# New duration estimates and earlier weight loads in the list schedule of a two-layer flow-matching backbone

## Chip, cores and metric

The kernel runs on one NeuronCore of a Trainium2 chip. The metric is the time of one execution on the device in microseconds (us), the median of several runs; lower is better. The engines are named as in the profile: PE multiplies matrices, DVE and ACT work on vectors and activations, POOL is hardly used, and SP issues every transfer (DMA) of the kernel.

## The reference

Two layers work on 1024 latent tokens and 256 context tokens of width 1024, in float32. Cut to what matters here:

```python
for l in range(DEPTH):                       # DEPTH = 2
    mod = silu(c) @ w_ada[l] + b_ada[l]      # shift, scale, gate; mod_c the same from c_ctx
    h  = rmsnorm(x,  norm_g[l]) * (1 + scale)   + shift
    hc = rmsnorm(xc, norm_g[l]) * (1 + scale_c) + shift_c
    if l % 2 == 1: h = to_col_major(h)       # the 64-wide grid, column by column
    p  = h  @ w_in[l]                        # 1024 x 3600
    pc = hc @ w_in[l]                        # last layer: only the columns of group A
    o_ctx, s_f, s_b = gdn_bidir(pc[..., :A_COLS], 0, 0, ...)
    o_lat, _, _     = gdn_bidir(p[..., :A_COLS], s_f, s_b, ...)
    y = mixer_output(o_lat, p, ...)          # groups A to D, gated, then @ w_out[l]
    x = x + gate * y                         # and xc likewise, but not in the last layer
return rmsnorm(x, final_g)
```

`gdn_bidir` is group A, a gated DeltaNet run forwards and backwards. In chunks of 64 tokens it forms, for each head, a 64x64 lower triangular matrix, inverts it (`tinv`), and then scans over the chunks with a 64x64 state. Group B is a short convolution, group C a convolution of 31 taps with a LayerNorm, group D a gate that mixes the tokens within chunks of 128.

## The kernel before

**Dense work.** Most of PE's time goes to `h @ w_in` and to the output projection, in tiles of 128x128 by 512 columns. The operands are split into a high and a low part, so that each product of a latent tile takes three matmuls (high by high, high by low, low by high). In the names of the trace `hh` and `hl` are the two parts of h, `w` holds the two parts of a block of weights, `r` is the raw block of 512 KB as it was loaded, and `mm` is the accumulator in PSUM. ACT casts `r` into the high part of `w`, DVE subtracts to get the low part. There are two buffers for `r` and two for `w` (`CAPS`); the blocks of the context rows are split into `u` buffers as well. The generator `dense` (its inner function `pump`) loads blocks ahead and splits them, in an order that the strings `ORDER` (layer 0) and `ORDER1` (layer 1) give.

**Group A.** For each set of chunks, PE forms the products of the pair matrices (accumulators `sc` and `ax`, constant operands `Lf` and `Lb`, one for each direction), DVE and ACT bring them into form in `b` buffers, and SP stores them to a scratch in DRAM (`zd`) in many small transfers. The inversion reads them back (`u<-zd`) with another layout and solves row by row on DVE: an alternation of `b<-u` and `u<-u,b`, whose width grows from 30 to 240 columns and shrinks again. There are two groups of it in the latent part. The result goes out to `zb`, comes back as `b<-zb`, is transposed, and `ax<-b,b` on PE begins the preparation of the scan (`ax_1275` in layer 1). The scan then runs chunk by chunk. Group D's gate has `u_1256<-u_1105` shuffles, small transfers from one buffer into another.

**What sets the order.** No instruction is issued where it is written. The whole program is recorded through stand-ins of the engines (`Engine`, `Program.add`), 11,657 operations, and `Program.schedule` puts them in order. It goes through time with one clock for each engine, takes the engine that can start an operation first and there, among the operations that are ready by its own reckoning, the one with the lowest priority number. That number is the place in the written program less a boost (`nc.boost`): 800 for the scan, 600 for the convolutions and for the split of weights (`AHEAD_SPLIT`), 300 for the pair matrices (`AHEAD_GDN`), 0 for the inversion (`AHEAD_INV`). The durations come from `estimate`; an issue on SP has a fixed price in `Program.add`. Some operations may go to ACT or DVE; the schedule chooses by its own clocks. Buffers are granted in the order of the program. Then the operations are emitted, and each engine works them off strictly in that order. Since all of them are issued by one call in `add`, every instruction has that line in the profile (L215).

Of the kernel before, what the change touches and what calls it, by code (L numbers as in the profile page):

```python
# [46 lines left out]
AHEAD_SCAN, AHEAD_GDN, AHEAD_INV, AHEAD_CONV, AHEAD_H, AHEAD_SPLIT = 800, 300, 0, 600, 0, 600  # L47
# [32 lines left out]
class Program:  # L80
# [60 lines left out]
    def estimate(self, eng, method, out, ins, args, kw):  # L141
        acc = kw.get("accum_out") is not None
        n = max(self.cols(out), max([self.cols(x) for x in ins[:1]] or [0]))
        ps = any(str(x.space) == "MemoryType.PSUM" or "PSUM" in str(x.space) for x in ins)
        ptr = sum(1 for x in ins if self.cols(x) == 1) if n > 1 else 0
        if eng == "PE":
            if method == "transpose":
                return 0.12
            lhsT, rhs = ins[0], ins[1]
            n, m, k = self.cols(rhs), self.cols(lhsT), lhsT.shape[0]  # L150
            if "r" in str(rhs.dtype).split("float32")[-1]:
                return max(0.107, n / 2400.0 + 0.0133)
            if m <= 64 or k <= 64:
                return max(0.116, 0.01 + n * 4 / 2400.0) / (4 if self.quads else self.side_by_side(k, m))
            return max(0.214, n * 4 / 2400.0) if n > 16 else 0.4
        if eng == "ACT":
            return (0.051 if ps else 0.093) + n / 1200.0 + 0.093 * (ptr + acc)
        if eng == "DVE":
            if method == "reciprocal":
                return 0.07 + n * 0.00625  # L160
            if method in ("tensor_scalar", "tensor_copy") and not ps:
                return 0.069 + n / 1920.0 + 0.06 * ptr
            return 0.069 + n / 960.0 + 0.06 * ptr
        if method == "memset":
            return 0.036 + n * 0.00083
        return 0.15 + n * 0.0021
# [20 lines left out]
    def add(self, calls):  # L187
        isap = lambda x: hasattr(x, "ap") and hasattr(x, "offset")
        eng, method, f, args, kw = calls[0]
        aps = lambda args, kw: ([args[0]] + ([kw["accum_out"]] if kw.get("accum_out") is not None else []),  # L190
                                [x for x in args[1:] if isap(x)] +
                                [v for k, v in kw.items() if k != "accum_out" and isap(v)])
        outs, ins = aps(args, kw)
        op = Op()
        i = len(self.ops)
        op.prio, op.users, op.ready, op.need, op.finish = i + self.boost, [], 0.0, 0, None
        op.alts, op.dma, op.area, op.mode = {}, 0.0, 0.0, None
        if eng == "PE":
            side = lambda x: 32 if x <= 32 else 64 if x <= 64 else P
            op.mode, op.area = (P, P), 1.0  # L200
            if method != "transpose":
                k, m = side(ins[0].shape[0]), side(self.cols(ins[0]))
                op.mode, op.area = (k, m), k * m / (P * P) * self.side_by_side(k, m)
        if eng == "SP":
            n = args[0].size() if callable(args[0].size) else args[0].size
            run = min(x.ap[-1][1] if x.ap[-1][0] == 1 else 1 for x in (args[0], args[1]))
            op.dma = n * 4 / 360e3 * (1.0 if run >= 128 else 2.0)
        for e, m, fn, ar, k in calls:
            table = None
            if e == "ACT" and m == "activation":  # L210
                func = ar[2] if len(ar) > 2 else k.get("func")
                table = self.TABLE.get(str(func).split(".")[-1])
            o, n = aps(ar, k)
            cost = 0.475 if e == "SP" else self.estimate(e, m, o[0], n, ar, k)
            op.alts[e] = ((lambda fn=fn, ar=ar, k=k: fn(*ar, **k)), cost, table)  # L215
        deps, tiles = set(), set()
        for w, aps in ((False, ins), (True, outs)):
            for a in aps:
                name = a.name
                if "PSUM" in str(a.space):  # L220
                    m = self.region(a)[2]
                    lo, hi = ((m & -m).bit_length() - 1) // 512, (m.bit_length() - 1) // 512
                    reg = (0, 128, (2 << hi) - (1 << lo))
                elif name in self.slots or "DRAM" in str(a.space):
                    if name not in self.slots and not name.startswith(self.DRAM_OWN):
                        continue
                    reg = self.region(a)
                else:
                    continue
                if name in self.slots:  # L230
                    tiles.add(name)
                h = self.hist.setdefault(name, [])
                keep = []
                for e in h:
                    j, jw, (p0, p1, m) = e
                    if j == i:
                        keep.append(e)
                        continue
                    hit = p0 < reg[1] and reg[0] < p1 and (m & reg[2])
                    if hit and (w or jw):  # L240
                        deps.add(j)
                        if w and reg[0] <= p0 and p1 <= reg[1] and not (m & ~reg[2]):
                            continue
                    keep.append(e)
                keep.append((i, w, reg))
                self.hist[name] = keep
        if self.joined is not None and eng == "PE":
            deps.add(self.joined)
            self.joined = None
        op.deps, op.tiles = deps, sorted(tiles)  # L250
        for t in tiles:
            self.tileops.setdefault(t, []).append(i)
        self.ops.append(op)
# [213 lines left out]
class Block:  # L467
# [375 lines left out]
    def dense(self, items):  # L843

        n = len(items)
        raws, ws = {}, {}
        st = {"l": 0, "s": 0}

        def pump(i):
            while True:  # L850
                s, moved = st["s"], False
                if s < min(i + 4, n) and s in raws:
                    it = items[s]
                    if self.room(it.pool)():
                        w = self.take(it.pool, [P, 2] + it.shape, F32R)
                        self.nc.boost -= AHEAD_SPLIT
                        self.split(w[:, 0], w[:, 1], raws.pop(s))
                        self.nc.boost += AHEAD_SPLIT
                        self.free("r")
                        ws[s] = w  # L860
                        st["s"] += 1
                        moved = True
                q = st["l"]
                if q < min(i + 6, n) and self.room("r")() and (items[q].cond is None or items[q].cond()):
                    raws[q] = r = self.take("r", [P] + items[q].shape)
                    items[q].load(r)
                    st["l"] += 1
                    moved = True
                if not moved:
                    return  # L870

        for i, it in enumerate(items):
            pump(i)
            while i not in ws:
                yield lambda: (st["l"] > i or items[i].cond is None or items[i].cond()) and \
                    (i not in raws or self.room(it.pool)())
                pump(i)
            for k, v in enumerate(it.run(ws[i])):
                if k % 8 == 0:
                    pump(i)  # L880
                yield v
            del ws[i]
            self.free(it.pool)
# [1285 lines left out]
```

## Time and profile before

| | before |
|---|---|
| median of 3 runs | 1415.69 us (1413.28 to 1418.06) |
| profiled execution | 1418.21 us |
| its span | 1416.1 us, so 2.1 us lie around it |
| mean granted clock of TensorE | 0.943 |
| PE, DVE, ACT busy | 1277.3, 986.6, 544.9 us |
| instructions on DVE; on ACT | 2112; 917, of them 87 table loads |

PE is busy for 90% of the span. Its idle time, 139 us, lies in a few places: the start up to 40 us, the context part of layer 0 (80 to 165 us), the middle of layer 0 where its inversion and scan start (420 to 520 us), and the same place of layer 1 (1090 to 1170 us). Elsewhere PE runs nearly without a gap. The granted clock is given as a share of 2.4 GHz; 0.5 is the lower level, 1.2 GHz.

### The profile page before, as it was taken

How to read it: one execution, taken by the hardware profiler on the slowest of the kernel's cores; microseconds unless marked ns; L12 is line 12 of the kernel's file. 1: busy time of each engine (PE TensorE's matmuls, PEld its weight loads, DVE VectorE, ACT ScalarE, POOL GpSimd, SP SyncE). 2: the span in 40 equal slices, each digit the busy share in tenths (PEclk: the TensorE clock that was granted, in tenths of full speed). 3: DMA queues.
4: the chain of work that ended last, by engine and by line, in shares of the span. 5: the costliest groups of instructions: out<-in, count | busy, mean ns of one | idle time of the engine just before them, and what ended most of it. 6: DMA issues, size and time to landing. Idle time of an engine off the chain costs nothing.

```text
span 1416.1 us, 27022 instructions
## 1 busy us (share of the span) xinstructions
PE 1277.3 (90%) x10888; PEld 1003.2 (71%) x10888; DVE 986.6 (70%) x2112; ACT 544.9 (38%) x917; POOL 11.9 (1%) x76
## 2 busy tenths in 40 slices
PE   6886699999988899999998999989998759999997
PEld 3875577986766655568886778978666646678886
DVE  4787969998855755573376669899776677784454
ACT  3876632254633122132154444343455303231221
POOL 1000000000000000000000000000000000000000
PEclk9997799999996889999999999999999779999999
DMA  9646332322447466573233332334226535132832
GB/s 310 182 108 183 108 89 62 88 46 58 104 105 172 121 178 193 179 223 104 90 112 109 114 104 63 67 81 101 62 50 147 136 85 127 51 105 89 262 84 56
DMA packets 310386, 166.75 MB, mean 118 GB/s; under 512 B 150174, under 2 KB 294902, under 8 KB 310262
## 3 DMA queue, kind: packets, MB, share of 16 engines
q1 hardware_dynamic: 310262, 165.03, 42.9%
q8 instruction: 85, 1.39, 0.4%
q14 instruction: 39, 0.32, 0.1%
HBM read 124.32 MB, written 35.42 MB: 113 GB/s over the span
## 4 chain that ended last, share of the span: by engine, by line
PE 52%; DVE 20%; DMA 12%; SPq 7%; ACT 5%; issue 4%; DVEq 0%; ACTq 0%; POOL 0%; POOLq 0%
PE mm L215 37%; DVE u L215 10%; PE sc L215 10%; SPq L215 7%; PE ax L215 5%; DVE b L215 5%; DMA x<-u 3%; DMA r<-in_w_in 3%; DVE w L215 2%; ACT b L215 1%; DMA u<-zd 1%; ACT L215 1%; DMA zd<-b 1%; ACT u L215 1%; DMA u<-in_x 1%
## 5 line engine op out<-in xcount | busy, mean ns | idle before, releaser
L215 PE MATMUL mm<-hh,w 128*128 128x512 f32 x1664 | 553.9, 407 | 6.8 <-ACT g L215 4.2
L215 PEld LDWEIGHTS mm<-hh,w 128*128 128x128 f32 x1664 | 316.1, 192 | 92.0 <-issue 20.8
L215 PE MATMUL mm<-hl,w 128*128 128x512 f32 x832 | 338.8, 407 | 1.5 <-issue 1.5
L215 PE MATMUL mm<-u,w 128*128 128x512 f32 (+1 forms) x1320 | 264.9, 359 | 13.9 <-ACT w L215 8.7
L215 PEld LDWEIGHTS mm<-u,w 128*128 128x128 f32 x1320 | 222.0, 195 | 48.1 <-ACT w L215 8.9
L215 DVE SCALAR_TENSOR_TENSOR u<-u,pv,u 128x1024 f32<-128x1024 f32 (+1 forms) x172 | 202.7, 1187 | 1.3 <-ACT u L215 0.6
L215 PEld LDWEIGHTS mm<-hl,w 128*128 128x128 f32 x832 | 159.9, 192 | 41.1 <-issue 9.4
L215 ACT CAST w<-r 128x1024 fp32r<-128x1024 f32 x88 | 92.5, 1052 | 249.5 <-PE mm L215 177.0
L215 DVE TENSOR_TENSOR w<-r,w 128x1024 fp32r<-128x1024 f32 x88 | 107.5, 1222 | 40.1 <-ACT w L215 39.8
L215 ACT ACT_TABLE_LOAD x87 | 111.6, 1283 | 21.4 <-DMA zd<-b 11.3
L215 DVE TENSOR_TENSOR u<-u,b 128x256 f32<-128x256 f32 (+26 forms) x246 | 90.1, 387 | 28.1 <-DMA u<-in_x 17.9
L215 ACT ACTIVATE b<-u 128x512 f32<-128x512 f32 (+1 forms) x71 | 42.5, 610 | 66.5 <-DVE u L215 45.5
L215 PE MATMUL mm<-u,u 128*128 128x256 f32 (+1 forms) x384 | 58.7, 303 | 5.7 <-ACT u L215 4.3
L215 DVE TENSOR_TENSOR b<-u 128x198 f32<-128x198 f32 (+24 forms) x180 | 56.9, 331 | 8.5 <-DMA u<-zd 6.9
L215 PEld LDWEIGHTS mm<-u,u 128*128 128x128 f32 x384 | 52.0, 201 | 9.0 <-ACT u L215 4.7
L215 PE MATMUL sc<-ident,b 128*128 128x128 f32 (+1 forms) x139 | 27.5, 322 | 25.2 <-ACT b L215 10.2
L215 PE MATMUL mm<-u,hh 128*128 128x272 f32 x256 | 48.5, 289 | 0.0
L215 PEld LDWEIGHTS sc<-v,u 64*64 64x64 f32 x1184 | 34.4, 140 | 19.6 <-DVE v L215 11.2
L215 PE MATMUL sc<-v,u 64*64 64x64 f32 x1184 | 42.9, 228 | 5.0 <-issue 4.0
L215 ACT COPY v<-sc 128x256 f32<-128x256 f32 x36 | 13.4, 372 | 78.6 <-PE sc L215 69.4
L215 ACT ACTIVATE b<-sc,mod,modG 128x128 f32<-128x128 f32 x86 | 35.0, 456 | 19.4 <-PE sc L215 11.0
L215 PEld LDWEIGHTS sc<-ident,b 128*128 128x128 f32 (+1 forms) x139 | 18.9, 163 | 32.6 <-ACT b L215 13.5
(273 smaller groups left out, 1455.6 us busy)
## 6 DMA issues: line engine op xcount, KB each, us to landing
r<-in_w_in SPq DMA_DIRECT2D x90, 512.0 KB
u<-in_w_ada SPq DMA_DIRECT2D x16, 1024.0 KB
u<-in_x SPq DMA_DIRECT2D x16, 512.0 KB
r<-ylat SPq DMA_DIRECT2D x16, 512.0 KB
ylat<-g SPq DMA_DIRECT2D x24, 256.0 KB
u<-in_w_out SPq DMA_DIRECT2D x12, 512.0 KB
at<-b SPq DMA_DIRECT2D x36, 128.0 KB
u<-at SPq DMA_DIRECT2D x18, 256.0 KB
```

The source lines that it names most:

```text
L215: op.alts[e] = ((lambda fn=fn, ar=ar, k=k: fn(*ar, **k)), cost, table)
```

## The change

Two things change, and no operation is added or taken away. First, the durations that the schedule reckons with: an ACT instruction costs 0.155 or 0.19 us (from PSUM or not) plus its columns, where it cost 0.051 or 0.093; a one-column DVE instruction 0.155 us; a DVE `tensor_tensor` of 129 to 256 columns in SBUF 0.4 us; a PE transpose 0.11 us, or 0.03 for at most 64 rows, where it was 0.12; and an issue on SP 0.62 us, where it was 0.475. Second, the load of a raw block of weights is boosted by 600 places, as its split was already.

```diff
             if method == "transpose":
-                return 0.12
+                return 0.11 if ins[0].shape[0] > 64 else 0.03
...
         if eng == "ACT":
-            return (0.051 if ps else 0.093) + n / 1200.0 + 0.093 * (ptr + acc)
+            return (0.155 if ps else 0.19) + n / 1200.0 + 0.05 * ptr + 0.093 * acc
         if eng == "DVE":
+            if n == 1:
+                return 0.155
             if method == "reciprocal":
                 return 0.07 + n * 0.00625
+            if method == "tensor_tensor" and not ps and 128 < n <= 256:
+                return 0.4
...
-            cost = 0.475 if e == "SP" else self.estimate(e, m, o[0], n, ar, k)
+            cost = 0.62 if e == "SP" else self.estimate(e, m, o[0], n, ar, k)
...
                     raws[q] = r = self.take("r", [P] + items[q].shape)
+                    self.nc.boost -= AHEAD_SPLIT
                     items[q].load(r)
+                    self.nc.boost += AHEAD_SPLIT
```

The effect is a new order on every engine. 104 operations also change between ACT and DVE: DVE has 24 more in all, ACT 24 fewer, and the table loads on ACT go from 87 to 81. Three places matter below, the third of them on two engines. In the names the first number is the buffer's own; the line is L215 before and L219 after, since four lines were added above it.

SP at the very start of the program, before (`whh` and `whl` are the halves of `w_ada`, `r_38` and `r_40` the first raw blocks of weights):

```order
1 L215 DMA b_6_99<-in_c 8x128
2 L215 DMA b_6_99<-in_c_ctx 8x128
3 L215 DMA whh_104<-in_w_ada 128x8x256 x2
4 L215 DMA u_11_106<-in_ctx 128x1024 x2
5 L215 DMA whh_104<-in_w_ada 128x8x256
```

and after:

```order
1 L219 DMA r_38_133<-in_w_in 128x4x16
2 L219 DMA r_38_133<-in_w_in 128x4x256
3 L219 DMA r_40_135<-in_w_in 128x4x16
4 L219 DMA r_40_135<-in_w_in 128x4x256
5 L219 DMA b_6_99<-in_c 8x128
6 L219 DMA b_6_99<-in_c_ctx 8x128
7 L219 DMA whh_104<-in_w_ada 128x8x256 x2
8 L219 DMA u_11_106<-in_ctx 128x1024 x2
9 L219 DMA whh_104<-in_w_ada 128x8x256
10 L219 DMA r_42_137<-in_w_in 128x8x128
```

The first two blocks (four transfers, 1.1 MB) went from behind the third load of `whl` to the head of the queue, and `r_42` and `r_44` (512 KB each) from behind all of `w_ada` to a place ahead of six of its eight loads.

SP in the context part of layer 0, around the loads of `r_201` and `r_210`, before:

```order
52 L215 DMA zd_175_272<-b_176_273 64x2x64 x2
53 L215 DMA zd_175_272<-b_183_280 128x2x64
54 L215 DMA zd_175_272<-b_183_280 64x2x64 x2
55 L215 DMA u_118_215<-u_118_215 32x4x32 x6
56 L215 DMA u_85_182<-in_x 128x1024
57 L215 DMA r_201_298<-in_w_in 128x8x128
58 L215 DMA r_210_307<-in_w_in 128x8x128
```

and after:

```order
46 L219 DMA r_180_277<-in_w_in 128x8x128
47 L219 DMA r_201_298<-in_w_in 128x8x128
48 L219 DMA r_210_307<-in_w_in 128x8x128
49 L219 DMA u_85_182<-in_x 128x1024
50 L219 DMA zd_175_272<-b_176_273 128x2x64
51 L219 DMA zd_175_272<-b_176_273 64x2x64
```

The two loads now stand ahead of the first stores of pair matrices; single issues counted, they moved forward by 29 places.

SP at the end of the pair matrices of layer 1, before the change (`zd_1187` and `zd_1214` are the scratch of the first and second inversion group):

```order
448 L215 DMA u_1186_1285<-zd_1187_1286 32x32x32
449 L215 DMA r_1252_1351<-in_w_in 128x8x128
450 L215 DMA u_1256_1355<-u_1105_1204 32x16x32 x2
451 L215 DMA u_1186_1285<-zd_1187_1286 32x32x32
...
487 L215 DMA zd_1214_1313<-b_1241_1340 64x2x64
488 L215 DMA u_1271_1370<-at_1185_1284 128x512
489 L215 DMA zd_1214_1313<-b_1241_1340 64x2x64
490 L215 DMA u_1186_1285<-zd_1214_1313 32x32x32
```

and after:

```order
477 L219 DMA zd_1214_1313<-b_1241_1340 64x2x64 x2
478 L219 DMA u_1186_1285<-zd_1187_1286 32x32x32 x2
479 L219 DMA r_1278_1377<-in_w_in 128x8x128
480 L219 DMA b_1274_1373<-zd_1187_1286 32x8x32 x4
481 L219 DMA u_1186_1285<-zd_1187_1286 32x32x32 x2
482 L219 DMA u_1256_1355<-u_1105_1204 32x16x32 x8
483 L219 DMA u_1186_1285<-zd_1214_1313 32x32x32 x2
```

The four loads of the first inversion group and eight shuffles of group D stood among the stores of the second group; with one `ylat` store these thirteen issues now stand behind the last store, so that both inversion groups get their data at the end.

PE at the last set of pair matrices of layer 1, before:

```order
3185 L215 MATMUL sc_1235_1334<-b_1237_1336,Lf_15_110 128x256
3186 L215 MATMUL sc_1235_1334<-b_1237_1336,Lb_16_111 128x256
3187 L215 MATMUL mm_1269_1368<-hl1_941,w_1251_1350 128x512
3188 L215 MATMUL mm_1269_1368<-hh1_940,w_1251_1350 128x512
3189 L215 MATMUL mm_1279_1378<-hh1_940,w_1258_1357 128x512
```

and after:

```order
3209 L219 MATMUL mm_1308_1407<-hh1_940,w_1277_1376 128x512 x2
3210 L219 MATMUL sc_1235_1334<-b_1237_1336,Lf_15_110 128x256
3211 L219 MATMUL sc_1235_1334<-b_1237_1336,Lb_16_111 128x256
3212 L219 MATMUL mm_1308_1407<-hl1_941,w_1277_1376 128x512
3213 L219 MATMUL mm_1308_1407<-hh1_940,w_1277_1376 128x512 x2
```

All dense matmuls of the block `w_1258` and the first of `w_1277` now stand ahead of this set. Between its `Lb` product and the first product of `ax_1275` there were 122 dense matmuls of 512 columns, now there are 62; the place of `ax_1275` itself, counted in work ahead of it on PE, is the same.

## Rows read from the trace of the kernel before

**Rows 1.** The page: busy time of the engines, and the chain's shares by engine.
```profile
PE 1277.3 (90%) x10888; PEld 1003.2 (71%) x10888; DVE 986.6 (70%) x2112; ACT 544.9 (38%) x917; POOL 11.9 (1%) x76
...
PE 52%; DVE 20%; DMA 12%; SPq 7%; ACT 5%; issue 4%; DVEq 0%; ACTq 0%; POOL 0%; POOLq 0%
```

**Rows 2.** Windows: stretch, length, engines busy, granted clock, DMA share, GB/s.
```profile
0.00:40.00 40.00, 26.90 (x198) 16.05 (x199) 17.14 (x70) 16.46 (x33) 3.75 (x36) 1.00 0.97 304
...
400.00:440.00 40.00, 32.97 (x249) 25.89 (x249) 14.88 (x26) 10.99 (x13) 0.00 (x0) 0.81 0.50 109
440.00:480.00 40.00, 35.81 (x158) 28.51 (x157) 36.12 (x124) 10.43 (x14) 0.31 (x2) 0.85 0.64 169
480.00:520.00 40.00, 32.93 (x659) 21.51 (x657) 20.32 (x52) 8.70 (x21) 0.00 (x0) 0.79 0.55 140
...
1160.00:1200.00 40.00, 34.04 (x865) 26.25 (x866) 29.61 (x73) 13.06 (x28) 0.00 (x0) 0.85 0.49 125
```

**Rows 3.** PE timeline, context part: start, length, matmul, [idle before it <- releaser].
```profile
85.61 0.50 PE L215 MATMUL mm<-u,u 128*128 128x256 f32 x2 [3.10 <-ACT u L215]
...
120.34 0.80 PE L215 MATMUL mm<-u,w 128*128 128x256 f32 x2 [8.65 <-ACT w L215]
122.36 0.80 PE L215 MATMUL mm<-u,u 128*128 128x256 f32 x2 [1.23 <-ACT u L215]
```

**Rows 4.** SP timeline in the context part: start, length of the issues, transfers.
```profile
109.65 3.86 SPq L215 DMA_DIRECT2D u<-u  x6
...
114.19 1.06 SPq L215 DMA_DIRECT2D r<-in_w_in  x2
```

**Rows 5.** The chain that ended last: a load of weights at two places.
```profile
39.67 5.92 DMA r<-in_w_in
...
114.67 6.58 DMA r<-in_w_in
```

**Rows 6.** The window of 10 us behind the longest wait of the context part.
```profile
120.00:130.00 10.00, 8.43 (x57) 7.99 (x57) 8.05 (x21) 5.35 (x12) 0.00 (x0) 0.61 0.53 140
```

**Rows 7.** SP timeline at the start: the first loads of weights.
```profile
25.46 2.03 SPq L215 DMA_DIRECT2D r<-in_w_in  x4
```

**Rows 8.** PE timeline in layer 1, from the pair matrices to the scan's preparation.
```profile
1093.48 1.03 PE L215 MATMUL sc<-b,Lf 128*128 128x256 f32 x2 [4.98 <-DVE b L215]
...
1102.47 0.59 PE L215 MATMUL sc<-b,Lb 128*128 128x256 f32 x2
...
1103.83 0.62 PE L215 MATMUL mm<-hh,w 128*128 128x512 f32 x2
...
1104.52 0.62 PE L215 MATMUL mm<-hh,w 128*128 128x512 f32 x2
...
1161.56 1.18 PE L215 MATMUL ax<-b,b 32*32 32x32 f32 x64 [12.20 <-DVE b L215]
```

**Rows 9.** SP timeline in layer 1: last store of pair matrices, and what follows.
```profile
1122.79 0.58 SPq L215 DMA_DIRECT2D zd<-b  x1
1123.47 2.23 SPq L215 DMA_DIRECT2D u<-zd  x1
...
1130.88 3.35 SPq L215 DMA_DIRECT2D b<-zd  x4
```

**Rows 10.** The chain in layer 1: a load for the inversion.
```profile
1134.77 4.53 DMA u<-zd
```

**Rows 11.** DVE timeline, inversion: first group begins, second begins, first ends, second ends.
```profile
1106.42 0.21 DVE L215 TENSOR_TENSOR b<-u 128x30 f32<-128x30 f32 x1 [4.96 <-DMA u<-zd]
...
1139.33 0.21 DVE L215 TENSOR_TENSOR b<-u 128x30 f32<-128x30 f32 x1 [1.92 <-DMA u<-zd]
...
1149.32 0.23 DVE L215 TENSOR_TENSOR u<-u,b 128x58 f32<-128x58 f32 x1
...
1165.33 0.19 DVE L215 TENSOR_TENSOR u<-u,b 128x30 f32<-128x30 f32 x1
```

**Rows 12.** The page, costliest groups: an ACT activation of 512 columns.
```profile
L215 ACT ACTIVATE b<-u 128x512 f32<-128x512 f32 (+1 forms) x71 | 42.5, 610 | 66.5 <-DVE u L215 45.5
```

## The prediction

> **What bounds the kernel now.** The page comes first. PE is busy for 1277 of 1416 us, and the chain that ended last runs through PE for 52%, through DVE for 20%, through transfers and their issue for 19% [rows 1]. So for most of the span PE's own work is the bound, and a new order can only change the 139 us in which PE waits. Reordering does not shorten PE's work, except where it keeps the clock at its upper level.
>
> The windows tell where these waits are [rows 2]. At the start (0 to 40 us) PE is busy for 26.9 us, and the DMA engines are 97% busy at 304 GB/s: transfers set the pace there. In the middle of layer 0 (400 to 520 us) PE idles for 120 - 32.97 - 35.81 - 32.93 = 18.3 us, and the granted clock is 0.79 to 0.85, between the two levels of 1.2 and 2.4 GHz. The PE timeline then gives the waits of the context part one by one [rows 3]: 3.10, 8.65 and 1.23 us, 13.0 us together, each for a cast or split of a block of weights. The reader should see behind the 8.65 us a transfer that was issued too late. SP issued the two loads at 114.19 us, behind six shuffles that took 3.86 us, 0.64 us each [rows 4], and one load took 6.58 us on the chain [rows 5]. Behind that wait the granted clock over 10 us is 0.61 [rows 6].
>
> The last big wait is in layer 1. PE idles for 12.20 us ahead of the scan's preparation at 1161.56 us, for data that come out of the inversion [rows 8]. From there PE works nearly without a gap to the end, so the time of this one matmul decides the time of the kernel.
>
> **The change part by part.** No work is added or taken away, so each term below is a change of PE's idle time, or of the time of the matmul at 1161.56 us. The sum is made against the profiled execution (1418.2 us), which lies 2.5 us above the median of the runs.
>
> *Start.* Before, the first four transfers of weights were issued at 25.46 us [rows 7]. They now lead the queue. They are 1.1 MB, at 304 GB/s [rows 2] 3.6 us, by which the first part of w_ada comes later. Two more loads (1.05 MB, 3.4 us) go ahead of six of the eight loads of w_ada. On the other side the load that stood on the chain for 5.92 us at 39.67 us [rows 5] is long done. The ends are -2.3 us (3.6 less 5.9) and +7.1 us (both delays in full); I take +4, because everything of the first 40 us waits for w_ada, and the row with 97% says that no bandwidth is free.
>
> The Trainium skill, DMA: Bandwidth & Descriptors, section Queues, rings and completion order, says that each DMA engine takes descriptors in the order of its ring. By that rule what is first in the queue delays all behind it in full, and this part would cost the larger delay. The trace speaks for something in between: the load of 512 KB took 5.92 us where its bytes alone would take 1.7 at 304 GB/s, so transfers in flight share the engines.
>
> *Context part.* The two late loads move from behind the stores of pair matrices to before them, by 29 issues, and the three pairs after them by 12 to 40. Of the 13.0 us I take 10 away; the loads of the first wait, at 85.6 us, move less (17 issues). With the wait of 8.65 us goes the slow clock behind it: 8.43 us of work at 0.61 [rows 6] would take 5.1, so at most 3.3 us; I take 2, since part of that work waits for other things. The ends are 0 and 16.3 us.
>
> *Other gaps.* An activation of 512 columns takes 610 ns [rows 12]. The old formula reckons 0.093 + 512/1200 = 0.52 us, the new one 0.62; an issue on SP takes 0.64 [rows 4] where 0.475 was reckoned. The list placed work on PE where it thought that inputs were ready, and they were not. What a truer list can get back is at most the 18.3 us in 400 to 520 us and the 4.98 us at 1093 us [rows 8], 23.3 us in all, and possibly nothing, since the order of priorities that makes the chain late is as before. I take half, 12.
>
> Together PE reaches the last pair matrices of layer 1 by D = 10 + 2 + 12 - 4 = 20 us earlier, if the work ahead of them were the same.
>
> *It is not the same.* Sixty more dense matmuls stand ahead of the last set of pair matrices. From 1103.83 to 1104.52 us three of them ran [rows 8], so one takes 0.23 us and sixty 13.8. The set's product, at 1102.47 us, moves to 1102.5 + 13.8 - 20 = 1096.3. The last store ended at 1123.4 us [rows 9]; thirteen other issues leave the queue ahead of it, 13 x 0.63 = 8.2 us, so it ends at 1123.4 + 13.8 - 20 - 8.2 = 1109.0. This takes the whole saving on SP, which is right as long as SP is what the stores wait for; the other end is none of it.
>
> Now the loads of the first inversion group come, which before had been issued among the stores. The first waits 2.2 us for the stores to land, four loads of b take 3.35 [rows 9], and four issues more at 0.6; the last lands 4.5 us later [rows 10], so 12.3 us in all, and the inversion starts at 1121.3. The second group took from 1139.33 to 1165.52 us, 26.2 us, while the first finished beside it [rows 11]; the first took 43.1 us (1106.42 to 1149.55), but with other work of DVE between its rows. I take 26.2, because the two groups will again run beside each other with little else: 1147.5 us. From the end of the first group to the matmul it was 1161.56 - 1149.55 = 12.0 us. So the matmul comes at 1159.5 us, **2 us earlier** than before, and the wait ahead of it grows from 12 to some 30 us: this is where most of D is lost again.
>
> *Behind it.* The second group's loads come some 9 us after the first's, so it is done at about 1156.5 instead of 1165.5 us. Between 1160 and 1200 us PE idles for 6.0 us [rows 2], 1.6 of them ahead of that matmul; I take 3 of the other 4.4 away. DVE's 24 more operations cost nothing where DVE has idle time, as it has here (29.6 us busy of 40 in the same row); without that cover they would cost their 9 us.
>
> The sum is -2 - 3 = -5 us: 1418.2 - 5 = 1413.2 for a profiled execution, and 2.5 less for the median, **1411 us**. In short, the change is 18 - D - 3 us, and D carries the doubt. Its own range is 1404 to 1418.
>
> **The rivals.**
>
> *The inversion becomes the bound, slower.* Its loads have no boost, and now stand behind all stores; both groups get their data at the end, with DVE's extra operations between their rows. If the inversion takes 35 us, midway between 26.2 and 43.1, the matmul comes 9 us later than in my sum; if besides only 8 us of D arrive (the context part alone), it is 12 us more: 1411 + 21 = 1432 us. For it: the wait of 12.2 us is already there, and cover of 13.8 us was taken from it. Against it: the first group's 43 us were stretched by waits for stores, which are over by then. It decides as soon as D is under 15 us with the inversion as I took it, since then 18 - D - 3 is positive.
>
> *The gaps close, much faster.* If the list's new durations are close enough, all 23.3 us of the other gaps go, and the context part gives its full 16.3: D = 23.3 + 16.3 - 4 = 35.6, and the time is 18 - 35.6 - 3 = -20.6, so 1395 us. For it: the two places in question are those where SP and ACT were reckoned too cheap. Against it: the other gaps lie on a chain of transfers and DVE rows that no order shortens.
>
> *The boost does nothing.* There are two buffers for raw blocks, and a load can't be issued before the split of the block two places before. Then the loads wait in the queue instead of at its end, the context part and the start give 0, and D = 12: 18 - 12 - 3 = +3, 1419 us. Against it: the order shows 29 places of difference at just the loads that were late.
>
> **How the numbers follow.** A measurement of this kernel tells about 0.3% (4.2 us) from no change. I give the forecast 0.35, the slow inversion 0.30, the closed gaps 0.20 and the boost without effect 0.15. Faster by more than 4.2 us means under 1411.4: over half of the forecast's cases (0.19), all of the closed gaps (0.20) and a little of the rest (0.03), 0.42. Within 0.3%: 0.14 of the forecast, 0.10 of the boost without effect, 0.02 of the slow inversion, 0.26. Slower: 0.28 of the slow inversion, 0.02 of the forecast and 0.02 of the boost without effect, 0.32. The range reaches from the closed gaps to the slow inversion, 1393 to 1434 us, and leaves about 1 in 10 on either side.
>
> **What would show it.** In the profile after: the first load of w_ada lands some 4 us later; the waits of PE for casts in 80 to 130 us add up to 3 us instead of 13.0, and the granted clock in 120 to 130 us is over 0.9; PE idles for under 10 us in 400 to 520 us; the first inversion of the latent part of layer 1 starts near 1121 us, behind the last store, and takes 26 us; the wait ahead of the scan's preparation there is near 30 us, and its first matmul comes at about 1160 us. If that wait is no longer than before, the cover was not lost and the time is lower; if the inversion takes over 35 us or the waits of 400 to 520 us are still there, the time is higher, and my D was wrong.

## The result and the profile after

The change made the kernel slower: 1430.59 us (median of 4 runs, 1426.17 to 1433.87) against 1414.62 us for the kernel before in the same runs, a ratio of 1.0104 (95% interval 1.0075 to 1.0134). The forecast was 1411 us and faster. The time lies in the range and near the rival "the inversion becomes the bound" (1432 us).

The profiled execution of after took 1426.17 us, its span is 1424.5 us, 8.4 us over that of before. The first lines of its page, busy time and chain by engine, answer to [rows 1]:

```profile
PE 1268.4 (89%) x10888; PEld 1000.1 (70%) x10888; DVE 991.9 (70%) x2136; ACT 524.2 (37%) x887; POOL 11.9 (1%) x76
...
PE 61%; DVE 16%; DMA 10%; SPq 6%; ACT 4%; issue 3%; ACTq 0%; DVEq 0%
```

PE's share of the chain rose from 52 to 61% while the kernel became slower. PE is not better fed by that: its idle time went from 139 to 156 us, while its busy time fell by 8.9 us. The idle time now stands in fewer and larger waits. The windows of after show where, beside [rows 2]:

```profile
0.00:40.00 40.00, 20.01 (x132) 11.12 (x132) 16.89 (x60) 15.54 (x26) 3.84 (x36) 0.91 1.00 309
400.00:440.00 40.00, 26.02 (x248) 21.59 (x246) 15.53 (x32) 6.76 (x10) 0.00 (x0) 0.77 0.53 125
440.00:480.00 40.00, 24.73 (x96) 19.86 (x96) 32.38 (x109) 7.24 (x9) 0.22 (x2) 0.80 0.48 118
480.00:520.00 40.00, 35.15 (x605) 24.54 (x607) 20.29 (x58) 8.45 (x19) 0.00 (x0) 0.87 0.59 161
1080.00:1120.00 40.00, 38.34 (x279) 30.34 (x278) 14.76 (x24) 10.25 (x15) 0.00 (x0) 0.89 0.55 125
1120.00:1160.00 40.00, 7.55 (x49) 4.98 (x47) 35.09 (x123) 1.54 (x3) 0.51 (x6) 0.54 0.42 91
1160.00:1200.00 40.00, 30.98 (x701) 23.86 (x701) 26.35 (x63) 10.98 (x24) 0.00 (x0) 0.80 0.44 101
1200.00:1240.00 40.00, 37.61 (x838) 26.67 (x840) 23.89 (x57) 7.71 (x17) 0.00 (x0) 0.83 0.23 70
```

At the start PE is busy for 20.0 us where it was 26.9. In 400 to 520 us it idles for 34.1 us, where it was 18.3. In 1120 to 1160 us, where DVE inverts, PE works for 7.6 us of 40; before it was 23.6. PE's timeline of after names four of the waits there, among them the longest three behind the start:

```profile
423.19 0.71 PE L219 MATMUL sc<-s,u 64*64 64x64 f32 x16 [5.17 <-DVE b L219]
...
450.18 0.79 PE L219 MATMUL mm<-hh,w 128*128 128x512 f32 x1 [17.82 <-ACT g L219]
...
1133.84 1.12 PE L219 MATMUL sc<-ident,b 128*128 128x128 f32 x4 [8.12 <-DMA b<-in_smlp_w]
...
1164.96 1.08 PE L219 MATMUL ax<-b,b 32*32 32x32 f32 x64 [28.62 <-DVE b L219]
```

The last row answers to the 12.20 us of [rows 8]: the wait ahead of layer 1's scan preparation has more than doubled, and the matmul behind it comes 3.4 us later. The SP timeline of after shows why, beside [rows 9]:

```profile
1108.46 4.27 SPq L219 DMA_DIRECT2D zd<-b  x5
1112.77 1.32 SPq L219 DMA_DIRECT2D u<-zd  x2
1114.19 0.65 SPq L219 DMA_DIRECT2D r<-in_w_in  x1
1114.95 2.06 SPq L219 DMA_DIRECT2D b<-zd  x4
1117.05 1.67 SPq L219 DMA_DIRECT2D u<-zd  x2
1118.77 6.54 SPq L219 DMA_DIRECT2D u<-u  x8
1125.41 1.34 SPq L219 DMA_DIRECT2D u<-zd  x2
```

The stores end at 1112.7 us, 10.7 us earlier than before. But all four loads of the first inversion group are behind them, where before they had been issued between 1080 and 1101 us. DVE's timeline shows what follows from that:

```profile
1123.79 0.20 DVE L219 TENSOR_TENSOR b<-u 128x30 f32<-128x30 f32 x1
...
1135.11 0.50 DVE L219 TENSOR_TENSOR b<-u 128x30 f32<-128x30 f32 x2 [2.14 <-DMA u<-zd]
...
1145.12 0.67 DVE L219 TENSOR_TENSOR b<-u 128x220 f32<-128x220 f32 x2
1145.70 0.67 DVE L219 TENSOR_TENSOR u<-u,b 128x220 f32<-128x220 f32 x2
...
1156.24 0.51 DVE L219 TENSOR_TENSOR u<-u,b 128x30 f32<-128x30 f32 x2
```

The first group starts 17.4 us later than before (1106.42 us, [rows 11]) and ends at about 1156.3 us. At 1135.11 us the second group begins; from there each row marked x2 is one row of either group, under the width of the first of them.

The wait of 17.82 us in layer 0 looks like the same pattern with another victim: PE waits for ACT to empty an accumulator into a `g` buffer. ACT waits for a `g` buffer, which comes free when SP has stored it (`gd<-g`). On SP, in the timeline of after, that store stands behind shuffles and the loads of the inversion:

```profile
437.93 2.63 SPq L219 DMA_DIRECT2D u<-u  x4
440.65 2.81 SPq L219 DMA_DIRECT2D u<-zd  x4
443.50 0.83 SPq L219 DMA_DIRECT2D gd<-g  x1
```

The store itself is not late against before, where the first such store was issued at 443.31 us and PE waited for the same buffer:

```profile
448.60 0.80 PE L215 MATMUL mm<-hh,w 128*128 128x512 f32 x1 [4.19 <-ACT g L215]
```

The matmul comes only 1.6 us later in after. The wait is 13.6 us longer because nothing covers it: from 427 to 444 us PE of before ran 17 dense matmuls of 512 columns, in after it ran none from 418 to 450 us.

### The profile page after: what moved, and what is told of

It reads as the page before. It is cut to its first block, busy times and chain, and to the rows that moved or that the text cites. A ratio compares the mean times of both kernels' runs of the same rounds, so it can differ in the third digit from the quotient of the medians.

```text
span 1424.5 us, 27030 instructions
## 1 busy us (share of the span) xinstructions
PE 1268.4 (89%) x10888; PEld 1000.1 (70%) x10888; DVE 991.9 (70%) x2136; ACT 524.2 (37%) x887; POOL 11.9 (1%) x76
## 4 chain that ended last, share of the span: by engine, by line
PE 61%; DVE 16%; DMA 10%; SPq 6%; ACT 4%; issue 3%; ACTq 0%; DVEq 0%
PE mm L219 47%; PE sc L219 10%; DVE u L219 8%; SPq L219 6%; PE ax L219 5%; DVE b L219 4%; DMA x<-u 3%; DVE w L219 2%; ACT b L219 2%; DMA r<-in_w_in 2%; DMA u<-in_x 1%; DMA u<-in_ctx 1%; ACT u L219 1%; DVE hl L219 1%; ACT w L219 1%
## 5 line engine op out<-in xcount | busy, mean ns | idle before, releaser
L219 PE MATMUL mm<-hh,w 128*128 128x512 f32 x1664 | 550.3, 406 | 27.8 <-ACT g L219 17.8
L219 PEld LDWEIGHTS mm<-hh,w 128*128 128x128 f32 x1664 | 314.8, 192 | 111.5 <-issue 19.2
L219 PE MATMUL mm<-hl,w 128*128 128x512 f32 x832 | 338.3, 407 | 0.0
L219 PE MATMUL mm<-u,w 128*128 128x512 f32 (+1 forms) x1320 | 261.7, 355 | 4.7 <-ACT u L219 3.4
L219 PEld LDWEIGHTS mm<-u,w 128*128 128x128 f32 x1320 | 218.4, 191 | 38.9 <-ACT u L219 4.0
L219 DVE SCALAR_TENSOR_TENSOR u<-u,pv,u 128x1024 f32<-128x1024 f32 (+1 forms) x172 | 202.2, 1183 | 1.5 <-ACT u L219 0.6
L219 PEld LDWEIGHTS mm<-hl,w 128*128 128x128 f32 x832 | 159.4, 192 | 41.0 <-issue 8.9
L219 ACT CAST w<-r 128x1024 fp32r<-128x1024 f32 x88 | 92.4, 1050 | 234.2 <-PE mm L219 176.8
L219 DVE TENSOR_TENSOR w<-r,w 128x1024 fp32r<-128x1024 f32 x88 | 107.3, 1219 | 44.9 <-ACT w L219 44.6
L219 ACT ACT_TABLE_LOAD x81 | 103.9, 1283 | 25.9 <-DMA gd<-g 14.8
L219 DVE TENSOR_TENSOR u<-u,b 128x512 f32<-128x512 f32 (+28 forms) x246 | 87.3, 378 | 27.6 <-DMA u<-in_x 17.2
L219 ACT ACTIVATE b<-u 128x512 f32<-128x512 f32 (+1 forms) x71 | 42.5, 609 | 69.2 <-DVE u L219 54.6
L219 PE MATMUL mm<-u,u 128*128 128x256 f32 (+1 forms) x384 | 56.5, 300 | 7.2 <-DVE u L219 3.6
L219 DVE TENSOR_TENSOR b<-u 128x30 f32<-128x30 f32 (+24 forms) x180 | 54.5, 323 | 8.1 <-DMA u<-zd 6.5
L219 PEld LDWEIGHTS mm<-u,u 128*128 128x128 f32 x384 | 51.4, 201 | 10.0 <-DVE u L219 4.6
L219 PE MATMUL sc<-ident,b 128*128 128x128 f32 (+1 forms) x139 | 27.5, 335 | 32.2 <-DVE b L219 11.0
L219 PE MATMUL mm<-u,hh 128*128 128x272 f32 x256 | 48.7, 289 | 0.5 <-DVE u L219 0.5
L219 PEld LDWEIGHTS sc<-ident,b 128*128 128x128 f32 (+1 forms) x139 | 20.4, 173 | 39.8 <-issue 16.4
L219 DVE TENSOR_TENSOR u<-u,mm 128x512 f32<-128x512 f32 (+1 forms) x30 | 18.9, 631 | 41.2 <-PE mm L219 41.0
L219 PE MATMUL ax<-b,b 32*32 32x32 f32 x1280 | 18.2, 203 | 32.6 <-DVE b L219 28.6
L219 PEld LDWEIGHTS sc<-v,u 64*64 64x64 f32 x1184 | 34.3, 141 | 13.9 <-DVE v L219 6.0
L219 PE MATMUL sc<-v,u 64*64 64x64 f32 x1184 | 42.7, 228 | 1.0 <-DVE v L219 0.8
```

## The experiments

Three theories were to be told apart. **Late inversion**: the loss is made in layer 1, where the inversion's loads stand behind all stores. **Late start**: the weight loads ahead of `w_ada` cost their time to the end. **Layer 0**: the wait of 17.8 us there is what counts. Each ratio is to runs of the kernel before on the same chip.

**The boost alone.** The durations are those of before.

```diff
-            return (0.155 if ps else 0.19) + n / 1200.0 + 0.05 * ptr + 0.093 * acc
+            return (0.051 if ps else 0.093) + n / 1200.0 + 0.093 * (ptr + acc)
...
-            cost = 0.62 if e == "SP" else self.estimate(e, m, o[0], n, ar, k)
+            cost = 0.475 if e == "SP" else self.estimate(e, m, o[0], n, ar, k)
```

> Only the boost of the weight loads; all durations as before. In its order the start and the context part are as in the change, layer 1 has the order of before (the first inversion group's loads among the stores, the pair matrices at the same places on PE), and layer 0's inversion loads stand behind the stores as in the change. Theory 'late inversion' (the loss is made where layer 1's inversion loads stand behind all stores): the time is 1408 to 1416 us, the wait ahead of layer 1's scan preparation 12 to 20 us. Theory 'late start' (the weight loads at the head of the queue delay w_ada, and that delay is carried to the end): 1420 us or more, the loss in the first 40 us still there at the end.

Measured: 1.0032 (1.0002 to 1.0061), slower by a little. The wait ahead of layer 1's scan preparation is 13.9 us, as expected; the median of 1422.9 us is over what the first theory said and lies where late start put it (1420 us or more). But late start also asked that the loss of the first 40 us be carried to the end, and PE ended layer 0 some 3 us ahead of before. The loss came behind that.

**The durations alone.** The two lines of the boost are taken out.

> Only the new durations; the loads of weights not boosted. The start is as before, layer 1 as in the change. 'Late inversion': 1428 to 1438 us, since the wait of some 28 us ahead of layer 1's scan preparation stays and the context part's gain is missing. 'Late start': 1414 to 1420 us.

Measured: 1.0126 (1.0076 to 1.0177), with a wait of 28.1 us. That is as late inversion has it. The early loads at the start are absent here, and the loss is as large.

**The inversion boosted by 300.**

```diff
-AHEAD_SCAN, AHEAD_GDN, AHEAD_INV, AHEAD_CONV, AHEAD_H, AHEAD_SPLIT = 800, 300, 0, 600, 0, 600
+AHEAD_SCAN, AHEAD_GDN, AHEAD_INV, AHEAD_CONV, AHEAD_H, AHEAD_SPLIT = 800, 300, 300, 600, 0, 600
```

> The change, and AHEAD_INV 300 in place of 0, so the inversion has the boost of the pair matrices. The first group's loads then stand 34 stores earlier on SP, and layer 0's as well. 'Late inversion': 1408 to 1418 us, the wait ahead of layer 1's scan preparation under 18 us, the wait of 17.8 us in layer 0 under 8. A rival, 'DVE is the limit there': the inversion's rows only take DVE's time from other work, and the time stays at 1425 to 1432 us.

Measured: 0.9979 (0.9954 to 1.0004), a median of 1411.74 us, as late inversion has it. The wait in layer 1 is 14.8 us, in layer 0 13.7 us (expected under 8).

**The first four blocks of weights not boosted.**

```diff
-                    self.nc.boost -= AHEAD_SPLIT
+                    ahead = AHEAD_SPLIT if q > 3 else 0
+                    self.nc.boost -= ahead
                     items[q].load(r)
-                    self.nc.boost += AHEAD_SPLIT
+                    self.nc.boost += ahead
```

> The change, with the first four blocks of weights not boosted: they stand where they stood before, behind w_ada. Layer 1 as in the change. 'Late start': 1418 to 1424 us. 'Late inversion': 1426 to 1432 us, since up to 7 us won at the start are lost again in the wait ahead of layer 1's scan preparation or are paid back by the context part.

Measured: 1.0096 (1.0061 to 1.013), with a wait of 28.6 us. The late start falls: with the start of before the loss is the same.

**Old durations of PE, ACT and DVE**, with the boost and SP's new price.

> The boost and the SP price of 0.62, with the old durations of PE, ACT and DVE. Layer 1's first inversion loads stand behind all stores here too, at the same places of the SP queue as in the change. Theory 'SP's price' (the price of an issue alone moves the inversion loads behind the stores, and that makes the loss): ratio 1.007 to 1.013 to before, a wait of 25 us or more ahead of layer 1's scan preparation. Rival 'ACT and DVE durations' (the loss comes from the other new prices): ratio under 1.004, the wait under 18 us.

Measured: 1.0008 (0.999 to 1.0027). The wait is 27.4 us, so SP's price does move the inversion loads; the loss did not come. Both expectations are half missed. PE's timeline of this run shows the wait as large as in the change and 13 us earlier:

```profile
1151.86 1.08 PE L215 MATMUL ax<-b,b 32*32 32x32 f32 x64 [27.39 <-DVE b L215]
```

PE came to the end of layer 0 with a lead that paid for the wait; the table below puts numbers to this.

**The inversion boosted in layer 1 alone.** Up to layer 1 the order is that of the change.

```diff
-                self.W.spawn(1 if gi == 0 else 2, self.boosted(AHEAD_INV, self.invert(st, gi)))
+                self.W.spawn(1 if gi == 0 else 2, self.boosted(300 if l else AHEAD_INV, self.invert(st, gi)))
```

> The change, with the boost of 300 for the inversion in layer 1 alone. Up to layer 1 the order is that of the change. Theory 'late inversion in layer 1': the ratio to before falls from 1.010 to 0.993 to 0.999, the wait ahead of layer 1's scan preparation to about 15 us, and layer 0's wait of 17.8 us is untouched. Rival 'layer 0 makes the loss' (the wait of 17.8 us in layer 0 is what counts): the ratio stays over 1.005.

Measured: 0.9968 (0.995 to 0.9985). This one edit takes the loss away and more. On SP the four loads stand among the stores again, in its timeline:

```profile
1086.64 1.31 SPq L219 DMA_DIRECT2D u<-zd  x2
1088.04 1.08 SPq L219 DMA_DIRECT2D at<-b  x2
1089.17 0.45 SPq L219 DMA_DIRECT2D zd<-b  x1
1089.66 1.49 SPq L219 DMA_DIRECT2D u<-zd  x2
1091.19 6.84 SPq L219 DMA_DIRECT2D zd<-b  x8
```

and its PE timeline has the matmul 13.6 us earlier than the change, with half of the wait:

```profile
1151.41 1.17 PE L219 MATMUL ax<-b,b 32*32 32x32 f32 x64 [14.78 <-DVE b L219]
```

The wait in layer 0 is still 17.6 us, so the loss can go without a mend of layer 0, and the time follows the place of the inversion's loads in layer 1. That their place behind all stores is what makes the change slower than before is not shown by this run alone: it would have to win more here than on the kernel before, where the loads were not behind all stores. That run follows below.

**The stores of the gates boosted by 600** (around the `gd` store in `group_a_gates`).

```diff
+                        self.nc.boost -= AHEAD_SPLIT
                         nc.sync.dma_start(st.gd[r:r + HD, b0:b0 + n], g[q * HD:(q + 1) * HD])
+                        self.nc.boost += AHEAD_SPLIT
```

> The change, with the stores of group A's gates (gd from g) boosted by 600; in layer 0 four of them move from behind the inversion loads to among the stores of pair matrices. Theory 'late inversion in layer 1': the wait of 17.8 us in layer 0 falls under 8 us, but the ratio stays at 1.006 to 1.012, since layer 1 is as in the change. Rival 'layer 0 makes the loss': 0.995 to 1.003.

Measured: 1.0072 (1.0048 to 1.0097). That is in the range of late inversion, but its interval overlaps that of the change. In PE's timeline the wait in layer 0 shrinks less than expected, a new one of 11.9 us follows it, and layer 1's stays. So this run moved layer 0's waits more than it removed them:

```profile
456.04 0.80 PE L219 MATMUL mm<-hh,w 128*128 128x512 f32 x1 [10.58 <-ACT g L219]
...
481.28 1.22 PE L219 MATMUL mm<-hh,w 128*128 128x512 f32 x2 [11.90 <-DVE w L219]
...
1160.07 1.07 PE L219 MATMUL ax<-b,b 32*32 32x32 f32 x64 [28.70 <-DVE b L219]
```

**The three mends together** (inversion of layer 1, gate stores, first four blocks).

> The change with three mends together: inversion of layer 1 boosted by 300, gate stores boosted by 600, and the first four blocks of weights not boosted. If the terms add (layer 1 some -15 us against the change, layer 0 -5, the start -2), the ratio to before is 0.990 to 0.996 and the kernel beats both. If PE's waits only move on to the next place, it is 0.996 to 1.002.

Measured: 0.9881 (0.986 to 0.9903), a median of 1397.61 us. This beats both kernels, and by a little more than the sum of the terms had it.

**The boost and the new durations of PE, ACT and DVE, with SP's old price.**

> The boost and the new durations of PE, ACT and DVE, with the old price of 0.475 for an issue on SP. The first inversion loads of layer 1 stand between the places of before and of the change (four issues, two of them 35 and two of them 9 behind the last store of the first group's scratch as before, 15 to 30 ahead of the second group's last store). Theory 'ACT and DVE prices cost by themselves' (the run with the old ones was 1.0008, the change 1.0104): ratio 1.004 to 1.012 although SP's price is old. Rival 'SP's price is needed for the loss': 0.997 to 1.003, with a wait of 12 to 18 us ahead of layer 1's scan preparation.

Measured: 1.0057 (1.0036 to 1.0078), with a wait of 22.7 us. The ratio is in the range of the first theory, that ACT and DVE prices cost by themselves; the next run tests that. The loads are partly late here, and so is the matmul, so the wait is not that of the rival either.

**The three mends with the old durations of PE, ACT and DVE.**

> The three mends (inversion of layer 1 boosted, gate stores boosted, first four blocks of weights not boosted) with the boost of the loads and SP's new price, and the old durations of PE, ACT and DVE. If the new ACT and DVE prices cost by themselves, as the run with the old ones suggests (10 us less than the change), this is 5 to 10 us faster than the three mends with all new prices: ratio to before 0.981 to 0.986. If what the old prices won lay in the same waits that the mends remove, 0.986 to 0.992.

Measured: 0.9922 (0.9899 to 0.9946). The new prices of ACT and DVE do not cost by themselves: without them the mended kernel is not faster. If anything it is slower by 0.4%, with intervals that just overlap. What the run with old ones had won did not add.

**The kernel before, with the inversion of layer 1 boosted** (the same one line).

> The kernel before, with the inversion of layer 1 boosted by 300 and nothing else. Theory 'late inversion in layer 1': its loads stand together behind the first group's stores, the wait of 12.2 us stays or grows by some us as cover moves ahead, and the time falls by 4 to 10 us (0.993 to 0.997), since the inversion begins some 15 us earlier. Rival 'the boost helps only where the loads had been pushed behind all stores': 0.998 to 1.003.

Measured: 0.9878 (0.9852 to 0.9904), 1398.49 us. One line makes the kernel before as fast as the three mends make the change, more than expected. In its PE timeline no wait is left at the matmul, against the expectation; dense work runs up to it:

```profile
1150.92 0.39 PE L215 MATMUL mm<-hh,w 128*128 128x512 f32 x1
1151.24 0.75 PE L215 MATMUL ax<-b,b 32*32 32x32 f32 x64
```

This run limits what late inversion explains. The boost takes 1.2% off the kernel before and 1.4% off the change (1.0104 to 0.9968), nearly the same. With it in both, the change is still the slower one, 0.9968 against 0.9878. So the place of four loads behind all stores does not by itself account for the 1.0%; what goes with the time in either kernel is how early the inversion starts, as the table below has it. The rival of this run falls.

**The three mends with all old durations.**

> The three mends and the boost of the loads from the fifth block on, with every duration as before the change. It differs from the three mends with all new durations (ratio 0.988) by the durations alone. If the new durations are of worth once the inversion is mended, this one is slower: 0.991 to 0.998. If they are not, and the inversion's place makes the gain, 0.983 to 0.990, as the kernel before with the inversion boosted alone (0.988).

Measured: 0.994 (0.9916 to 0.9964), against 0.9881 with all the new ones. So with these three mends the new durations are of worth, 0.6%. That does not make them better in general: the kernel before with one boost, and all old durations, is as fast as the best run with new ones (0.9878 beside 0.9881).

**What the runs have in common.** One matmul is the same in all of them: the transpose at 789.12 us of before, in the output projection of layer 0. In every run the profile has 4899 instructions of PE from there on. Its time tells with what lead PE goes into layer 1. The next column is how long after it the first row of layer 1's latent inversion starts on DVE. "To the end" is the span less the time of the matmul, and the last column compares that with before. Each row is a single profiled execution, and executions of one kernel lay 5 to 17 us apart, so differences of a few us between rows can be chance.

| run | that matmul, us | lead | from there to the inversion, us | to the end, us | against before |
|---|---|---|---|---|---|
| before | 789.1 | 0 | 317.3 | 627.0 | 0 |
| the change | 786.4 | 2.7 | 337.4 | 638.1 | +11.1 |
| boost alone | 786.1 | 3.0 | 325.4 | 637.0 | +10.0 |
| durations alone | 794.7 | -5.6 | 335.9 | 639.8 | +12.8 |
| first four blocks late | 792.4 | -3.2 | 337.7 | 632.4 | +5.4 |
| SP's price old | 792.1 | -3.0 | 328.0 | 637.3 | +10.3 |
| PE, ACT, DVE old | 779.4 | 9.7 | 330.8 | 634.2 | +7.2 |
| gate stores | 783.4 | 5.8 | 335.7 | 635.6 | +8.6 |
| inversion 300 | 794.4 | -5.2 | 305.5 | 612.4 | -14.6 |
| inversion in layer 1 | 785.2 | 3.9 | 309.6 | 619.1 | -7.9 |
| three mends | 778.2 | 10.9 | 307.9 | 616.7 | -10.3 |
| mends, PE, ACT, DVE old | 799.4 | -10.3 | 296.0 | 605.0 | -22.0 |
| mends, all old | 779.1 | 10.0 | 310.3 | 625.5 | -1.5 |
| before, inversion in layer 1 | 788.7 | 0.4 | 299.9 | 613.7 | -13.3 |

Every run without a boost of layer 1's inversion loses 5 to 13 us from there on, every run with it wins 1.5 to 22. The column of the inversion sorts them the same way: where it starts later than in before the stretch is longer, where it starts earlier it is shorter, without an exception. That holds for the boost alone too, whose inversion starts 8.1 us later although its loads stand among the stores, and for the boosted pair: 309.6 us in the change against 299.9 in before. The size follows only roughly, and other things differ between these orders, so this is a strong correlation and no proof.

The lead at the end of layer 0, on the other hand, lies anywhere between -10 and +11 us, whatever was changed. It explains why the run with old ACT and DVE durations came out even: its 9.7 us of lead paid for 7.2 us of loss. For the change it says that layer 0, with its wait of 17.8 us, was no slower than before: the lead is 2.7 us. That wait ate gain which I had forecast; it made no loss against before.

## Why the prediction was wrong

**Start: right in kind.** I took 4 us. PE's first matmul on `w_ada` began 4.0 us later (10.97 instead of 7.00 us), and at 40 us PE had been busy for 6.9 us less. In the times it can't be seen, as the run with the first four blocks late shows: 1.0096 beside 1.0104.

**Context part: right on the waits, not on the gain.** Of the 13.0 us of waits for casts [rows 3] at most 2.05 us are left between 80 and 130 us, and the clock in 120 to 130 us is 0.91 where it was 0.61 [rows 6]. In the PE timeline of after, beside one row of ACT, the first wait is still in the main for a cast, which could start only at 91.49 us, when its load had landed; the other two are for accumulators that ACT or DVE had to empty:

```profile
91.49 1.04 ACT L219 CAST u<-r 128x1024 fp32r<-128x1024 f32 x1 [2.02 <-DMA r<-in_w_in]
...
92.86 5.16 PE L219 MATMUL mm<-u,u 128*128 128x256 f32 x24 [2.05 <-ACT u L219]
105.20 3.13 PE L219 MATMUL mm<-u,u 128*128 128x256 f32 x24 [1.52 <-ACT u L219]
...
128.44 0.80 PE L219 MATMUL mm<-u,u 128*128 128x256 f32 x2 [3.62 <-DVE u L219]
```

But over 80 to 165 us PE's idle time fell only from 32.3 to 26.4 us, since other waits took the place of these. With the start's loss that leaves nothing: from 0 to 165 us PE idled for 49.7 us, before for 50.3, and with the new durations but no boost for 49.9.

**Other gaps: wrong.** I took half of the waits in 400 to 520 us away; they nearly doubled (34.1 us instead of 18.3). PE had run ahead through dense work, so it met layer 0's chain with less cover, as the wait for the `g` buffer shows above. At the end of layer 0 the lead was 2.7 us, where -4 + 12 + 9 = 17 stood in my sum (start, context part, half of the 18.3 us).

**D: right in sum, not in its parts.** The last set's product came at 1097.62 us, for which I had 1096.3. By my own 13.8 us of added work D is 18.7 us where I said 20. But 16 of it were won in layer 1 itself, in part where PE's waits ahead of that set closed: in 800 to 1080 us it idled for 5.0 us instead of 11.5, and the 4.98 us of [rows 8] are gone.

**The path to the matmul: 5.5 us too short.** Against my working, the stores ended at 1112.7 instead of 1109.0 us (+3.7: leaving SP's queue saved 5.9 us, not 8.2). The inversion began 11.1 us later instead of 12.3 (-1.2). It took 32.5 us instead of 26.2 (+6.3). From its end to the matmul it was 8.7 us instead of 12.0 (-3.3; some 0.7 of that is a misreading, since the row taken for the first group's end in before has 58 columns, and its last row of 30 came right behind it). **The step that failed is "I take 26.2, because the two groups will again run beside each other with little else".** The 26.2 us were read where wide rows of one group ran beside narrow rows of the other. In after both are wide at the same time, and a row of 220 columns with one of 210 takes 0.58 us from one pair to the next (1145.12 to 1145.70); a row of 220 alone took 0.42 to 0.43. From its rising row of 220 columns to its end the first group of after took 21.2 us, where the second group of before took 16.1 (+5.1). The rest lies ahead of that row (11.3 us instead of 10.1): at 1135.11 us DVE waited 2.1 us for the second group's load, because the second group's first row stands in DVE's order ahead of the first group's next one.

**"Behind it": wrong, by 8 us.** I took 3 us away from what follows the matmul, because the second group would be done earlier. It was (1163.4 instead of 1165.5 us), yet from the matmul to the end of the span it is 259.5 us where it was 254.5. The windows from the common matmul to this one, and from it to the end, show what the 5.0 us are; before:

```profile
789.12:1161.56 372.44, 335.19 (x2259) 270.78 (x2260) 288.41 (x577) 154.18 (x230) 3.93 (x18) 0.94 0.38 92
1161.56:1416.10 254.54, 238.16 (x2640) 189.64 (x2640) 150.17 (x312) 67.09 (x127) 0.00 (x0) 0.96 0.38 110
```

and after:

```profile
786.40:1164.96 378.56, 334.45 (x2259) 269.60 (x2259) 291.28 (x594) 146.61 (x221) 3.93 (x18) 0.92 0.38 91
1164.96:1424.50 259.54, 242.82 (x2640) 192.48 (x2640) 148.56 (x303) 65.87 (x123) 0.00 (x0) 0.94 0.37 107
```

Behind the matmul PE's idle time is 16.7 us, before 16.4, so none of the 3 us came. The same 2640 instructions were busy for 4.7 us longer, at a mean clock of 0.94 instead of 0.96: this term is a lower clock and not a wait. In 1160 to 1240 us the clock is 0.80 and 0.83; before it was 0.85 [rows 2] and then 0.96. Up to the matmul it is the other way round: PE was busy for as long as before, and all of the loss there is idle time (44.1 us instead of 37.3).

That the long wait ahead of the matmul brings the lower clock behind it is only argued, and the other runs bear it out at most roughly: with a wait of 27 to 29 us it is 255 to 262 us from the matmul to the end, with one under 15 us 251 to 257, and the run of the durations alone, with a wait of 28.1 us, has a mean clock of 0.97 there. One run stands apart with 264 us and no wait, the mends with old PE, ACT and DVE durations; there 45 more instructions of PE stand behind the matmul.

5.5 and 8 us are the distance from the 1413.2 us forecast to the 1426.2 us of the profiled execution, but for half a microsecond; the median of after lies 4.4 us higher still.

**The rivals.** "The inversion becomes the bound" names the place where it happened, but that its 1432 us is near the measured 1430.6 is luck. The inversion took 32.5 us instead of 35, D was 18.7 instead of 8, and 8 us came behind the matmul, where the rival had my gain of 3 us. Its deciding point was given wrongly for the same reason. "The gaps close" fell with the waits in 400 to 520 us. "The boost does nothing" fell in its mechanism, since the waits for casts closed. In the sum it is not refuted: start and context part cancel by 165 us, and boost and no boost with the new durations can't be told apart (1.0104 and 1.0126, with overlapping intervals).

What stays open: why the inversion of the boost alone started later with nearly the order of before in layer 1, why the change stays behind before when both have the boost of the inversion, what lowered the clock behind the matmul, and which part of re-sorting sets the lead at the end of layer 0.

## What to carry to other kernels

In a list schedule a truer price for one resource also changes who comes first on it. Before believing that it helps, look where the loads of the longest dependent chain now stand in each queue: here the start of one inversion, whose four loads had no boost, sorted fourteen runs of layer 1 into longer and shorter. A boost that repairs a change should also be tried on the kernel before, since here it was worth as much there. The work that PE does ahead of a chain is cover taken from its wait; a lead is lost again if the chain doesn't start earlier with it. And a duration read where two streams overlap holds only for the widths that overlapped there.

## What was not expected

- One line, a boost of 300 for layer 1's inversion, is worth 1.2% on the kernel before (0.9878), more than anything in the change.
- PE's lead at the end of layer 0 varied by 21 us between orders of the same work (778.2 to 799.4 us), although each changed only a few prices or boosts. These are single executions.
- PE's share of the chain that ended last rose by 9 points while its idle time rose by 17 us: the share tells where the chain ran, not how well PE is fed.
- Wide rows of the two inversion groups beside each other (220 and 210 columns) took 0.58 us a pair, so they still cost less than the 0.83 us or so of two alone, but more than the 0.43 us seen with narrow rows beside wide ones.
